# A decoder layer on one core: stores of h spread over more slots, v instead of silu multiplied by the norm factors on VectorE, form loads issued by SyncE

## The chip, the cores and the metric

The kernel runs on one core of one Trainium2 chip. The time is device microseconds of that core for one launch. The kernel before takes 2357.27 us, the median of 3 runs (2357.1 to 2358.58).

## What is computed

One layer of a hybrid decoder for 512 prompt rows and 8 sample rows (520 columns, held transposed: channels on partitions). A mixer (short convolution and gated linear attention) and its output projection come first; the change doesn't touch them. Then comes the ConvFFN, cut here to what matters:

```
xn = rmsnorm(x)                     # row factor R, gain g
u, v = split(xn @ w_up, 2)          # 2048 -> 2 x 5632
cu, new = causal_dwconv(u, prev, conv_w)   # width 3, over the rows
h = silu(cu + conv_b) * v
y = rmsnorm(x + h @ w_down)         # 5632 -> 2048
```

`new` is the last two rows of u (10 columns per channel here: 2 of the prompt and 8 samples), an output of its own.

## The kernel before, in words

**The stages.** Mixer and output projection run until about 866 us of the span, the up projection until 1867, the down projection until 2280, and the last four blocks of it with the final norm until 2356.

**Every product is in three parts.** A weight tile of 128 x 1024 numbers is split into `hi` (rounded, ScalarE, line 1045) and `lo` (the rest, VectorE, line 1049), and each activation into hi and lo as well; hi·hi, hi·lo and lo·hi are added up in PSUM. The tags `hi` and `lo` have three buffers each.

**Both projections use a fast 2 x 2 scheme with seven products.** Instead of eight block products there are seven, of sums of weight blocks and sums of input blocks ("forms"). `order` lists them: for each of 44 groups t of the up projection (128 channels of u and of v) the products r = 1, 5, 6, 2, 7, 3, 4, then for each of 5 chunks c of the down projection's inputs and 4 groups g of its outputs the same seven. One product is 24 matmuls. I call the time of one product a slot; a group has 7 slots, j = 0 to 6, and two groups, an even t and the odd one after it, are a pair.

**One pass of the loop (line 1301) is one slot.** In this order it emits: `up_finish` of the product just done; the 24 matmuls; `prepare(i + 2)`, which makes hi and lo of the product two slots ahead and, where needed, the next weight sum into `s` or `raw` (VectorE, line 1009); the steps of `gate` that are due. TensorE, VectorE and ScalarE keep this order (class InOrder); SyncE's and GpSimd's instructions are placed by the scheduler, and each of those queues then works in its order too. All weight loads (`raw`) are issued by SyncE.

**up_finish.** After r = 2, 3 the two halves of u go to `zpad`, multiplied by R (lines 1124 to 1129), and `keep_last` copies the last ten columns to `last` (line 521, on GpSimd); after every eleventh group `last` is transposed by TensorE and stored as `flat`. After r = 7 and 4 the two halves of v come out, negated (lines 1126 and 1132).

**gate(t)** is a generator that starts in the group after t; the number it yields is the slot, counted from its start, at which it goes on. Slot 0: the convolution (line 459 on ScalarE, lines 464 and 467 on VectorE). Slot 1: silu (line 1159, ScalarE), then silu times R on GpSimd (line 1160, by the helper at 219). Slot 3: h = v · s (line 1163). Slot 4, for odd t: the sums t21 and t34 of the quarters of two groups' h (lines 1175 to 1178). Then `stored` writes hi and lo of four tiles to DRAM: b11 (a half of the even group's h) at slot 8, t21 at 10, t34 and h both at 11. The last four groups are stored plain.

**stored (line 1134)** makes hi in a tile `fh` (ScalarE, line 116; two buffers) and lo in place (VectorE, line 117), and GpSimd issues both as DMAs to `f_d` (line 1144).

**The down projection** loads its forms from `f_d` (line 1208, four loads of 260 KB a form) and the residual (`acc`, line 1221), both issued by GpSimd. `load_form(0, 0..3)` stands in the last up group, 4 to 6 in the first down group, and the forms of chunk c + 1 in the last group of chunk c, one in each slot.

Of the kernel before, what the change touches and what calls it, by code (L numbers as in the profile page):

```python
# [9 lines left out]
F32 = mybir.dt.float32  # L10
F32R = mybir.dt.float32r
U8 = mybir.dt.uint8
AF = mybir.ActivationFunctionType
ALU = mybir.AluOpType
# [3 lines left out]
P = 128  # L18
D = 2048
KD = D // P  # L20
NP = 512
NS = 8
T = NP + NS
HT = T // 2
# [5 lines left out]
CH = 4  # L30
NCD = 5
# [6 lines left out]
def trunk_kernel(  # L38
# [6 lines left out]
    nc = tc.nc  # L45
# [7 lines left out]
    dp = ctx.enter_context(tc.tile_pool(name="scratch", bufs=1, space=DRAM))  # L53
# [31 lines left out]
    def tmp():  # L85
        return tp.tile([P, T + 2], F32, tag="t", name="t")

    def two(ap):
        return ap.rearrange("p (a b) -> p a b", a=2)
# [24 lines left out]
    def split(src, hi, lo, scale=None):  # L114
        if scale is None:
            nc.scalar.activation(hi, src, AF.Copy)  # L116
            nc.vector.tensor_tensor(lo, src, hi.bitcast(F32), op=ALU.subtract)  # L117
        else:
            nc.scalar.activation(hi, src, AF.Copy, scale=scale)  # L119
            nc.vector.scalar_tensor_tensor(  # L120
                lo, src, scale, hi.bitcast(F32), op0=ALU.mult, op1=ALU.subtract
            )
# [95 lines left out]
    def ptt(out, a, b, op):  # L218
        nc.gpsimd.tensor_tensor(out, a, b, op=op)  # L219
# [40 lines left out]
    with ExitStack() as es:  # L260
# [67 lines left out]
        ps = tps()  # L328
# [184 lines left out]
        zcount[0] += 1  # L513
        return zpad[zcount[0] % 2]

    def keep_last(z, j, n, new_p, new_s, get=bank):

        jj = j % n
        if jj == 0:
            last[0] = zp.tile([P, 10, n], F32, tag=f"last{n}", name="last", bufs=2)  # L520
        nc.gpsimd.tensor_copy(last[0][:, :, jj], z[:, NP:])
        if jj == n - 1:
            lt, c0 = last[0], (j - n + 1) * P

            def out():
                ps = get()
                nc.tensor.transpose(
                    ps[: 10 * n, :P], lt.rearrange("p r j -> p (r j)"), idn
                )
                flat = zp.tile([110, P], F32, tag="flat", name="flat", bufs=2)  # L530
                nc.scalar.activation(flat[: 10 * n, :], ps[: 10 * n, :P], AF.Copy)
                for r in range(10):
                    dst = new_p[0, 0, r] if r < 2 else new_s[0, r - 2, 1]
                    nc.sync.dma_start(
                        dst[c0 : c0 + n * P].rearrange("(j p) -> j p", p=P),
                        flat[r * n : (r + 1) * n, :],
                    )

            soon.append(lambda: None)
            soon.append(out)  # L540
# [512 lines left out]
    def minus(out, ps, x):  # L1053
        nc.vector.scalar_tensor_tensor(out, ps, -1.0, x, op0=ALU.mult, op1=ALU.subtract)  # L1054

    def add(out, x, y):
        nc.vector.tensor_tensor(out, x, y, op=ALU.add)
# [31 lines left out]
    def up_finish(i):  # L1089

        _, (t,), r = order[i]
        st = state[t,]
        bk = st["bank"]
        if r == 1:
            st["z"] = next_z()
        z1, z2 = st["z"][:, 2 : 2 + HT], st["z"][:, 2 + HT : 2 + T]
        if r == 7:
            st["v"] = tmp()
            v1, v2 = halves(st["v"][:, :T])
        if not t:  # L1100
            if r == 1:
                st["c"] = tmp()[:, :HT]
                nc.scalar.activation(st["c"], bk["a"], AF.Copy)
            elif r == 2:
                add(z1, bk["e"], st["c"])
            elif r == 6:
                st["u"] = halves(tmp()[:, :T])
                add(st["u"][0], bk["b"], st["c"])
            elif r == 7:
                u3 = st["u"][1]  # L1110
                add(u3, bk["b"], st["c"])
                minus(v2, bk["c"], u3)
                minus(v1, bk["d"], u3)
            elif r == 3:
                add(z2, bk["c"], st["u"][0])
        elif r == 1:
            copied(st, "e")
        elif r == 6:
            copied(st, "f")
        elif r == 5:  # L1120
            st["c"] = tmp()[:, :HT]
            nc.scalar.activation(st["c"], bk["c"], AF.Copy)
        elif r == 2:
            nc.vector.tensor_tensor(z1, bk["e"], R[:, :HT], op=ALU.mult)
        elif r == 7:
            minus(v2, bk["a"], st["c"])
        elif r == 3:
            add(z2, bk["f"], st["c"])
            nc.vector.tensor_tensor(z2, z2, R[:, HT:], op=ALU.mult)
            keep_last(st["z"], t, 11, new_ffn_p, new_ffn_s, mm_bank)  # L1130
        elif r == 4:
            nc.scalar.activation(st["v"][:, :HT], bk["a"], AF.Copy, scale=-1.0)

    def stored(src, dst):

        n = src.shape[1]
        hi = wxp.tile([P, T], F32R, tag="fh", name="fh")[:, :n]
        lo = src.bitcast(F32R)
        split(src, hi, lo)
        for d, x in zip(dst, (hi, lo)):  # L1140
            if len(d.shape) == 3:
                x = two(x)
                d = d.rearrange("f p c -> p f c")
            nc.gpsimd.dma_start(d, x)

    def gate(t):

        st = state.pop((t,))
        z, v = st["z"], st["v"]
        if not t:  # L1150

            nc.vector.tensor_tensor(z[:, 2 : 2 + T], z[:, 2 : 2 + T], R, op=ALU.mult)
            keep_last(z, t, 11, new_ffn_p, new_ffn_s, mm_bank)
        c = tmp()
        conv_tap(c, z, fcw, NF, t, fcb[:, t : t + 1])
        conv_rest(c, z, fcw, NF, t, stf[:, t, :])
        yield 1
        s = tmp()
        nc.scalar.activation(s[:, :T], c[:, :T], AF.Silu)  # L1159
        ptt(s[:, :T], s[:, :T], R, ALU.mult)  # L1160
        yield 3
        h = tmp()[:, :T]
        nc.vector.tensor_tensor(h, v[:, :T], s[:, :T], op=ALU.mult)
        yield 4
        if t >= NF - CH:
            stored(h, hl_d[t - NF + CH])
            return
        if t % 2 == 0:
            even[t] = h
            return  # L1170
        he, dst = even.pop(t - 1), f_d[t // 8]
        i = t // 2 % 4
        t21, t34 = tmp()[:, :T], tmp()[:, :T]
        (b11, b12), (b21, b22), (t2, t1), (t3, t4) = map(halves, (he, h, t21, t34))
        nc.vector.tensor_tensor(t1, b11, b12, op=ALU.subtract)
        minus(t2, t1, b22)
        nc.vector.tensor_tensor(t3, b22, b12, op=ALU.subtract)
        minus(t4, t2, b21)
        yield 8
        stored(b11, [dst[6, x, i] for x in range(2)])  # L1180
        yield 10
        stored(t21, [dst[0:2, x, i] for x in range(2)])
        yield 11
        stored(t34, [dst[2:4, x, i] for x in range(2)])
        stored(h, [dst[4:6, x, i] for x in range(2)])

    f_d = [dp.tile([7, 2, 4, P, HT], F32R, name=f"f_d{c}") for c in range(NCD)]
    hl_d = [[dp.tile([P, T], F32R, name=f"h{s}_d{t}") for s in "hl"] for t in range(CH)]
    even = {}


# [6 lines left out]
    def load_form(c, j):  # L1198

        home = (7 * c + j) % 8  # L1200
        parts_ = []
        for x in range(2):
            tiles = []
            for q in range(2):
                t = slots[2 * home + q].tile(
                    [P, T], F32R, tag=f"y{'hl'[x]}{2 * home + q}", name="form"
                )
                nc.gpsimd.dma_start(
                    two(t), f_d[c][PLACE[ORDER[j]], x, 2 * q : 2 * q + 2].rearrange("i p c -> p i c")
                )  # L1210
                tiles += halves(t)
            parts_.append(tiles)
        xd[c, ORDER[j]] = list(zip(*parts_))

    def load_residual(g):

        for q in range(4):
            m, b = 4 * g + 2 * (q // 2), q % 2
            n = 4 * g + q
            acc[g, q] = bigA.tile([P, T], F32, tag=f"x{'hl'[n % 2]}{8 + n // 2}", name="acc")  # L1220
            nc.gpsimd.dma_start(
                two(acc[g, q]),
                x1_d[m : m + 2, :, b * HT : (b + 1) * HT].rearrange("m p c -> p m c"),
            )

    def load_last():

        for i in range(CH):
            for b, (t0, n) in enumerate(PARTS):
                q = []  # L1230
                for x in range(2):
                    t = quarter(bigA, f"x{'hl'[x]}{2 * i + b}", QW)[:, :n]
                    nc.gpsimd.dma_start(t, hl_d[i][x][:, t0 : t0 + n])
                    q.append([t])
                hs[b].append(q)

# [243 lines left out]
```

## Time and profile before

| what | value |
|---|---|
| median of 3 runs | 2357.27 us |
| the profiled execution's own time | 2357.82 us |
| its span, first to last instruction | 2356.1 us |
| granted TensorE clock, mean of the span | 0.973 |
| up projection, 866 to 1867 us | 1001 us, TensorE busy 933.63 |
| down projection, 1867 to 2280 us | 413 us, TensorE busy 405.77 |
| GpSimd's multiplications by R (line 219, 44) | 4846 ns each |
| `last` copies on GpSimd (line 521, 52 of which 8 in the mixer) | 987 ns each |

Times in a view are counted from the span's start. A wait is put down to the engine and line whose event came last. TensorE's busy time overlaps with its weight loads (PEld). The granted clock is a share of full speed; a busy TensorE at half the clock does half the work.

### The profile page before, as it was taken

To read this page: it belongs to the slowest core of one execution; us is meant where nothing else is said; L and a number is where in the kernel's file an instruction comes from. 1 tells how busy PE (TensorE), PEld (TensorE's weight loads), DVE (VectorE), ACT (ScalarE), POOL (GpSimd) and SP (SyncE) were. 2 spreads that over 40 slices of the span, in tenths; PEclk is the share of its full clock that TensorE was granted. 3 is DMA by queue.
4 is the path that set the end of the run, shared out by engine and by line. 5 is a ranking of instruction groups with operands and counts; after the bars stand their busy time and mean duration, and the time that the engine had idled before them with its cause. 6 is when DMAs were issued, how large, how long until landed. Compare 5 with 4: busy or idle time off the path is not lost.

```text
span 2356.1 us, 43650 instructions
## 1 busy us (share of the span) xinstructions
PE 2245.6 (95%) x18131; PEld 2218.8 (94%) x18131; DVE 1627.4 (69%) x2124; ACT 1003.6 (43%) x1385; POOL 675.3 (29%) x642
## 2 busy tenths in 40 slices
PE   8999999999999999999999999999998899999996
PEld 7998999999999999999989999999998899999996
DVE  6446456343334468888888888878887787888885
ACT  5334434321223345444544545444454444444445
POOL 2113223100002222433433334343343632321410
PEclk9999999999999999999999999999999999999998
DMA  7443334333455453655565465464556988866834
GB/s 215 116 121 117 102 109 127 93 90 91 118 157 167 153 173 108 155 121 139 127 149 131 115 163 132 120 153 122 140 129 155 236 240 220 235 175 167 217 108 135
DMA packets 481539, 344.06 MB, mean 146 GB/s; under 512 B 17673, under 2 KB 463525, under 8 KB 481197
## 3 DMA queue, kind: packets, MB, share of 16 engines
q1 hardware_dynamic: 396193, 246.70, 37.3%
q0 software_dynamic: 83824, 92.34, 16.8%
q8 instruction: 142, 2.33, 0.4%
q10 hardware_dynamic: 1324, 2.23, 0.3%
q14 instruction: 56, 0.46, 0.1%
HBM read 278.15 MB, written 63.27 MB: 145 GB/s over the span
## 4 chain that ended last, share of the span: by engine, by line
PE 68%; DVE 11%; DMA 8%; issue 6%; ACT 4%; POOL 3%; SPq 0%; DVEq 0%; ACTq 0%; POOLq 0%
PE mm L133 31%; PE mm L1077 15%; PE x L1253 6%; PE y L1253 6%; DMA f_d<-fh 5%; DVE lo L1049 4%; PE f L1253 2%; PE e L1253 2%; PE ms L1077 2%; DVE s L1009 2%; POOL t L219 2%; ACT hi L1045 2%; DVE t L1054 1%; PE ms L717 1%; DMA raw<-in_w_in_dram 1%
## 5 line engine op out<-in xcount | busy, mean ns | idle before, releaser
L1077 PE MATMUL mm<-yh,hi 128*128 128x260 f32 x1408 | 416.1, 296 | 61.3 <-DVE t L1054 61.3
L1077 PE MATMUL mm<-yl,hi 128*128 128x260 f32 x1408 | 414.8, 295 | 1.0 <-DVE yl L117 1.0
L1077 PE MATMUL mm<-yh,lo 128*128 128x260 f32 x1408 | 413.0, 293 | 0.0
L1049 DVE TENSOR_TENSOR lo<-s,hi 128x1024 fp32r<-128x1024 f32 x192 | 260.3, 1356 | 128.6 <-ACT hi L1045 128.2
L1045 ACT ACTIVATE hi<-raw 128x1024 fp32r<-128x1024 f32 x256 | 270.4, 1056 | 172.9 <-issue 59.4
L1077 PEld LDWEIGHTS mm<-yh,hi 128*128 128x128 f32 x1408 | 280.8, 199 | 65.0 <-ACT hi L1045 65.0
L1049 DVE TENSOR_TENSOR lo<-raw,hi 128x1024 fp32r<-128x1024 f32 x256 | 319.2, 1247 | 19.4 <-ACT hi L1045 18.2
L104 ACT ACTIVATE hi<-raw 128x1024 fp32r<-128x1024 f32 (+1 forms) x148 | 152.8, 1034 | 391.4 <-PE mm L133 380.8
L105 DVE TENSOR_TENSOR lo<-raw,hi 128x1024 fp32r<-128x1024 f32 (+1 forms) x148 | 185.9, 1258 | 192.4 <-ACT hi L104 182.6
L133 PE MATMUL mm<-xh,hi 128*128 128x260 f32 (+2 forms) x1280 | 313.6, 294 | 5.0 <-ACT xh L119 2.6
L133 PE MATMUL mm<-xh,lo 128*128 128x260 f32 (+2 forms) x1280 | 303.6, 285 | 0.0
L133 PE MATMUL mm<-xl,hi 128*128 128x260 f32 (+2 forms) x1280 | 302.2, 284 | 0.8 <-DVE xl L120 0.5
L1077 PEld LDWEIGHTS mm<-yl,hi 128*128 128x128 f32 x1408 | 281.5, 200 | 1.3 <-DVE yl L117 1.2
L1077 PEld LDWEIGHTS mm<-yh,lo 128*128 128x128 f32 x1408 | 281.9, 200 | 0.0
L1045 ACT ACTIVATE hi<-s 128x1024 fp32r<-128x1024 f32 x192 | 203.1, 1058 | 184.0 <-DVE s L1009 102.0
L219 POOL TENSOR_TENSOR t<-t,R 128x520 f32<-128x520 f32 x44 | 213.2, 4846 | 142.3 <-ACT t L1159 142.2
L133 PEld LDWEIGHTS mm<-xh,hi 128*128 128x128 f32 x1280 | 216.9, 190 | 15.4 <-issue 9.2
L133 PEld LDWEIGHTS mm<-xl,hi 128*128 128x128 f32 x1280 | 217.4, 190 | 1.6 <-DVE xl L120 1.4
L133 PEld LDWEIGHTS mm<-xh,lo 128*128 128x128 f32 x1280 | 215.9, 189 | 0.1
L1077 PE MATMUL ms<-xh,hi 128*128 128x260 f32 x704 | 198.9, 282 | 2.1 <-ACT xh L116 2.1
L1077 PE MATMUL ms<-xl,hi 128*128 128x260 f32 x704 | 198.4, 282 | 0.5 <-DVE xl L117 0.5
L1077 PE MATMUL ms<-xh,lo 128*128 128x260 f32 x704 | 198.9, 283 | 0.0
(388 smaller groups left out, 5401.1 us busy)
## 6 DMA issues: line engine op xcount, KB each, us to landing
raw<-in_w_up_dram SPq DMA_DIRECT2D x176, 512.0 KB
raw<-in_w_down_dram SPq DMA_DIRECT2D x96, 512.0 KB
raw<-in_w_in_dram SPq DMA_DIRECT2D x92, 512.0 KB
form<-f_d POOLq DMA_DIRECT2D x140, 260.0 KB, 7.5
f_d<-fh POOLq DMA_DIRECT2D x60, 260.0 KB, 5.6
f_d<-t POOLq DMA_DIRECT2D x60, 260.0 KB, 4.2
raw<-in_w_out_dram SPq DMA_DIRECT2D x28, 512.0 KB
xT_d<-t SPq DMA_DIRECT2D x16, 260.0 KB
```

Source lines behind the costliest of these rows:

```text
L104: nc.scalar.activation(hi, raw, AF.Copy)
L105: nc.vector.tensor_tensor(lo, raw, hi.bitcast(F32), op=ALU.subtract)
L133: nc.tensor.matmul(o, w, xx, start=first and i == 0, stop=last and i == 2)
L219: nc.gpsimd.tensor_tensor(out, a, b, op=op)
L717: nc.tensor.matmul(pb[:, c * 64 : (c + 1) * 64], L[:, c, :], rhs[:, c], start=True, stop=True,)
L1009: return lambda: nc.vector.tensor_tensor(out, x, y, op=ALU.add)
L1045: nc.scalar.activation(his[i], src, AF.Copy)
L1049: nc.vector.tensor_tensor(los[i], src, his[i].bitcast(F32), op=ALU.subtract)
L1054: nc.vector.scalar_tensor_tensor(out, ps, -1.0, x, op0=ALU.mult, op1=ALU.subtract)
L1077: nc.tensor.matmul(st["bank"][b], w[:, k, :], x, start=b not in st["used"] and k == 0 and j == 0, stop=k == 7 and j == 2, skip_group_check ...
L1253: nc.tensor.matmul(ps[:, m, :], w[:, k, m * P : (m + 1) * P], x, start=b not in st["used"] and k == 0 and j == 0, stop=k == 3 and j == 2, ...
```

## The change

**v times R on VectorE.** GpSimd's `s = silu · R` goes. In slot 2 VectorE multiplies v by R in place (128 x 520), and in slot 3 it makes h = (v · -1) · s by a scalar_tensor_tensor in place of a tensor_tensor. The sign moved there, so that the two halves of v are now taken out of PSUM without negation.

**The copy to `last`** of the up projection goes from GpSimd to ScalarE (the mixer's eight stay on GpSimd).

**Stores.** h is stored at slot 15 of the gate, that is in slot 1 of the second group after, no longer at 11 right behind t34.

**Loads.** The scratch tensors have type F32 instead of F32R (the same bytes), and the forms and the residual are loaded by SyncE. The last four groups' tiles (line 1233) are still loaded by GpSimd.

```diff
+        if get:
+            nc.scalar.activation(last[0][:, :, jj], z[:, NP:], AF.Copy)
+        else:
+            nc.gpsimd.tensor_copy(last[0][:, :, jj], z[:, NP:])
...
-            minus(v2, bk["a"], st["c"])
+            add(v2, bk["a"], st["c"])
...
-            nc.scalar.activation(st["v"][:, :HT], bk["a"], AF.Copy, scale=-1.0)
+            nc.scalar.activation(st["v"][:, :HT], bk["a"], AF.Copy)
...
         nc.scalar.activation(s[:, :T], c[:, :T], AF.Silu)
-        ptt(s[:, :T], s[:, :T], R, ALU.mult)
+        yield 2
+        nc.vector.tensor_tensor(v[:, :T], v[:, :T], R, op=ALU.mult)
         yield 3
+
         h = tmp()[:, :T]
-        nc.vector.tensor_tensor(h, v[:, :T], s[:, :T], op=ALU.mult)
+        nc.vector.scalar_tensor_tensor(h, v[:, :T], -1.0, s[:, :T], op0=ALU.mult, op1=ALU.mult)
...
         stored(t34, [dst[2:4, x, i] for x in range(2)])
+        yield 15
         stored(h, [dst[4:6, x, i] for x in range(2)])
...
-                nc.gpsimd.dma_start(
-                    two(t), f_d[c][PLACE[ORDER[j]], x, 2 * q : 2 * q + 2].rearrange("i p c -> p i c")
+                nc.sync.dma_start(
+                    two(t.bitcast(F32)),
+                    f_d[c][PLACE[ORDER[j]], x, 2 * q : 2 * q + 2].rearrange("i p c -> p i c"),
                 )
...
-            nc.gpsimd.dma_start(
+            nc.sync.dma_start(
                 two(acc[g, q]),
```

Where it moves instructions, three places. First GpSimd's queue over one pair in the middle of the up projection; `fh` rows are stores of hi, `t` rows of lo, 128x260 is b11, and 128x2x260 are t21, t34 and h. Before:

```order
L521 COPY last<-zpad_880 128x10
L219 TENSOR_TENSOR t<-t,R 128x520
L521 COPY last<-zpad_881 128x10
L1144 DMA f_d_9533<-fh 128x260
L219 TENSOR_TENSOR t<-t,R 128x520
L1144 DMA f_d_9533<-t 128x260
L1144 DMA f_d_9533<-fh 128x2x260
L1144 DMA f_d_9533<-t 128x2x260
L1144 DMA f_d_9533<-fh 128x2x260 x2
L1144 DMA f_d_9533<-t 128x2x260 x2
```

And now:

```order
L1146 DMA f_d_9531<-fh 128x260
L1146 DMA f_d_9531<-t 128x260
L1146 DMA f_d_9531<-fh 128x2x260 x2
L1146 DMA f_d_9531<-t 128x2x260 x2
L1146 DMA f_d_9531<-fh 128x2x260
L1146 DMA f_d_9531<-t 128x2x260
```

Only the eight stores are left; no multiplication and no copy stands between them.

Second, ScalarE at the border of two groups, from the last hi of weights for the old group to the convolution of the next gate. `hi<-s` behind `last` belongs to r = 5 of the next group, the one behind `t<-mm` to r = 6. Before:

```order
L116 ACTIVATE fh<-t 128x520 x2
L1045 ACTIVATE hi<-raw 128x1024
L1045 ACTIVATE hi<-s 128x1024
L1132 ACTIVATE t<-mm 128x260
L1045 ACTIVATE hi<-s 128x1024
L459 ACTIVATE t<-zpad_880,parf 128x520
```

And now:

```order
L116 ACTIVATE fh<-t 128x520
L1048 ACTIVATE hi<-raw 128x1024
L522 ACTIVATE last<-zpad_880 128x10
L1048 ACTIVATE hi<-s 128x1024
L1135 ACTIVATE t<-mm 128x260
L1048 ACTIVATE hi<-s 128x1024
L459 ACTIVATE t<-zpad_880,parf 128x520
```

The `fh` of h has gone from behind that of t34, and the copy to `last`, which reads `zpad` after VectorE's multiplication by R, stands ahead of the hi of r = 5.

Third, SyncE's queue where the down projection begins. Before:

```order
L1005 DMA raw<-in_w_up_dram 128x8x128 x36
L1005 DMA raw<-in_w_down_dram 128x4x256 x7
L534 DMA out_dram<-flat 11x128 x10
L1005 DMA raw<-in_w_down_dram 128x4x256 x73
L94 DMA raw<-in_w_down_dram 128x4x256 x15
```

And now:

```order
L1008 DMA raw<-in_w_down_dram 128x4x256 x3
L1213 DMA form<-f_d_9530 128x2x260 x3
L1008 DMA raw<-in_w_down_dram 128x4x256
L1213 DMA form<-f_d_9530 128x2x260 x13
L1008 DMA raw<-in_w_down_dram 128x4x256
L537 DMA out_dram<-flat 11x128 x10
L1008 DMA raw<-in_w_down_dram 128x4x256 x3
L1227 DMA acc<-x_d 128x2x260 x4
L1213 DMA form<-f_d_9530 128x2x260 x12
L1227 DMA acc<-x_d 128x2x260 x4
L1008 DMA raw<-in_w_down_dram 128x4x256 x4
L1213 DMA form<-f_d_9531 128x2x260 x4
```

Forms and residual now stand between the weights; the fifth to seventh form of the first chunk stand behind the ten stores of `flat`, three weight loads and four residual loads.

## Prediction before the run

> **What bounds the kernel now.** I read the engines' totals first, then busy times by stage, then the chain that ended last, then the waits, and at last VectorE's own timeline over one pair. Totals, from the page:
>
> ```profile
> PE 2245.6 (95%) x18131; PEld 2218.8 (94%) x18131; DVE 1627.4 (69%) x2124; ACT 1003.6 (43%) x1385; POOL 675.3 (29%) x642
> ```
>
> TensorE is the bound, but 69% for VectorE is a mean over unlike stages. By stage (columns: us, busy times of PE, PEld, DVE, ACT, POOL, granted clock, DMA share, GB/s), the up and the down projection:
>
> ```profile
> 866.00:1867.00 1001.00, 933.63 (x7420) 928.80 (x7418) 836.64 (x1061) 489.06 (x672) 393.27 (x278) 0.96 0.56 136
> 1867.00:2280.00 413.00, 405.77 (x3366) 405.29 (x3367) 332.52 (x324) 173.36 (x190) 129.87 (x167) 0.99 0.74 201
> ```
>
> The down projection has little to give. The up projection has 67 us without a matmul, and its clock is below full. VectorE is busy there for 84%. The chain of work (start, us, what) shows the period: 20 stretches of this kind lie between these two starts, so 19 pairs take 864.63 us, 45.5 us each.
>
> ```profile
> 957.40 13.29 PE mm L1077 x96
> 1122.01 5.78 PE mm L1077 x48
> 1822.03 13.12 PE mm L1077 x96
> ```
>
> The middle row is undisturbed: 48 matmuls in 5.78 us, a slot of 2.89, so that TensorE alone needs 14 · 2.89 = 40.5 us a pair. 5.0 us a pair are lost. The chain in one pair shows where:
>
> ```profile
> 1260.51 0.65 ACT t L1159
> 1261.24 2.09 POOL t L219
> 1263.33 2.95 issue
> 1266.43 0.60 POOL f_d L1144
> 1267.03 7.31 DMA f_d<-fh
> 1274.42 0.65 ACT fh L116
> 1275.71 0.43 DVE t L1054
> 1276.28 14.46 PE mm L1077 x96
> ```
>
> GpSimd multiplies silu by R; the store of t21's hi queues behind that; it lands 7.3 us later; ScalarE, which wants t21's `fh` buffer for h, waits, and with it every hi behind it; VectorE and TensorE follow. The waits over the whole run (total, times, longest):
>
> ```profile
> ACT fh L116 <- DMA f_d<-fh: 106.9, 20, 6.4
> PEld mm L1077 <- ACT hi L1045: 65.0, 20, 4.2
> PE mm L1077 <- DVE t L1054: 63.5, 21, 4.0
> ```
>
> Twenty pairs, 3.25 us of idle TensorE each (the last two rows are the same time). The rest of the 5.0 is the clock:
>
> ```profile
> 1230.64:1276.28 45.64, 42.11 (x337) 41.92 (x337) 37.63 (x49) 21.92 (x30) 17.76 (x13) 0.95 0.57 134
> 1276.28:1322.79 46.51, 43.25 (x337) 43.07 (x337) 37.47 (x49) 21.70 (x30) 17.69 (x13) 0.94 0.55 131
> ```
>
> These are two pairs; 0.05 · 45.64 = 2.3 and 0.06 · 46.51 = 2.8 us of full-speed work are missing.
>
> **The change part by part.** *The stall goes.* Without the multiplication and with h four slots later, ScalarE wants t21's buffer 5 slots (14.4 us) after it was filled. The path is fh 0.65, issue 0.60, landing at most 7.31: 8.6 us. t34 wants b11's buffer after 3 slots, 8.7 us; b11 is half as large, so its path is shorter. The lo of h is read out until about 0.7 + 0.7 + 7.3 us after slot 1; the tile is wanted by v in slot 5, 11.5 us after. If all else had room, a pair would be 40.5 us.
>
> *VectorE becomes the next limit.* Rows of its timeline and ScalarE's, at the border of two groups and after (start, duration; in brackets its wait):
>
> ```profile
> 1300.36 0.43 DVE L1129 TENSOR_TENSOR zpad<-zpad,R 128x260 f32<-128x260 f32 x1
> 1300.71 1.22 DVE L1049 TENSOR_TENSOR lo<-s,hi 128x1024 fp32r<-128x1024 f32 x1
> 1301.96 1.23 DVE L1009 TENSOR_TENSOR s<-s,raw 128x1024 f32<-128x1024 f32 x1
> 1304.38 1.23 DVE L1049 TENSOR_TENSOR lo<-s,hi 128x1024 fp32r<-128x1024 f32 x1 [1.19 <-ACT hi L1045]
> 1305.52 0.75 DVE L464 SCALAR_TENSOR_TENSOR t<-zpad,parf,t 128x512 f32<-128x512 f32 x1
> 1312.29 2.07 DVE L1049 TENSOR_TENSOR lo<-s,hi 128x1024 fp32r<-128x1024 f32 x1 [0.21 <-ACT hi L1045]
> 1314.89 0.69 DVE L1163 TENSOR_TENSOR t<-t 128x520 f32<-128x520 f32 x1
> 1315.50 0.42 DVE L1124 TENSOR_TENSOR zpad<-ms,R 128x260 f32<-128x260 f32 x1
> ```
>
> ```profile
> 1303.28 1.06 ACT L1045 ACTIVATE hi<-s 128x1024 fp32r<-128x1024 f32 x1 [0.61 <-DVE s L1009]
> 1304.25 0.81 ACT L459 ACTIVATE t<-zpad,parf 128x520 f32<-128x520 f32 x1
> ```
>
> VectorE's busy time in this pair is 37.5 us (row 1276.28:1322.79 above; a union, overlaps counted once). Its path for a changed pair:
> - Less 0.85: the lo of 2.07 us ran beside GpSimd's multiplication, its like take 1.22.
> - Plus 2 · 0.61: v times R, priced by L1163 (same shape, two inputs in SBUF), from its start at 1314.89 to the next at 1315.50.
> - Plus 2 · 0.06: h as a scalar_tensor_tensor (L464 takes 0.75 for 512 columns, L1163 0.69 for 520).
> - Plus 2 · 1.19: the wait for the hi of r = 6, which needs s from VectorE; in each group, as now.
> - Plus 2 · 1.4, new: the copy to `last` on ScalarE. It reads what L1129 writes, and the hi of r = 5 is queued behind it; the lo of r = 5 is VectorE's next instruction. Today that lo starts while L1129 ends. Then it starts after a reaction of 0.09 (s ends at 1303.19, hi starts at 1303.28), the copy, a hi of 1.06 and 0.04 to the lo, less 0.09 overlap of ScalarE's instructions (1304.25 against 1304.34), with 0.08 more because VectorE's overlap is lost. The copy itself isn't in the trace on ScalarE; the nearest row is this one (columns: busy, mean ns):
>
> ```profile
> L635 ACT ACTIVATE asm<-t 128x8 f32<-128x8 f32 x4 | 0.8, 208 | 4.0 <-DVE t L627 4.0
> L521 POOL COPY last<-zpad 128x10 f32<-128x10 f32 x52 | 51.3, 987 | 224.0 <-DVE zpad L1129 220.1 <-DVE zpad L1152 3.5
> ```
>
> I take 0.21, for it has ScalarE's fixed part and almost the shape. The other end is GpSimd's 0.99 for the same copy.
>
> Sum: 37.5 - 0.85 + 1.22 + 0.12 + 2.38 + 2.8 = 43.2 us. VectorE never waits for TensorE on this path (its products run ahead of what it evacuates), so this is the period: 2.3 us a pair less than 45.5, times 20 = 46 us. With GpSimd's price for the copy the pair is 44.8 (14 us gained); with no new wait it is 40.5. Groups without the stores, at both ends, stay at TensorE's pace. Taking v without the negation costs nothing and brings nothing: the instructions stay, and 128x260 is 0.42 on VectorE with or without.
>
> *Where TensorE then waits.* 43.2 - 40.5 = 2.7 us a pair, in pieces of about 1 us, mostly in r = 2, whose lo comes behind the convolution. Do they lower the clock? The shortest stall of today's twenty didn't. Its wait, and the 7 us that hold it and the 7 us behind it:
>
> ```profile
> PE mm L1077 <- DVE t L1054: 1.7, 1, 1.7
> 1455.00:1462.00 7.00, 6.13 (x51) 6.17 (x52) 6.12 (x8) 2.77 (x4) 3.17 (x4) 1.00 0.73 166
> 1462.00:1469.00 7.00, 7.00 (x61) 7.00 (x59) 6.63 (x9) 5.01 (x9) 2.96 (x1) 1.00 0.17 47
> ```
>
> So at 1 us I count on full clock. The Trainium skill speaks against it: "TensorE: Matmul & The Clock Gate", section "A second HAM failure mode: psum-queue depth-cycling", says that frequent micro-idles between groups of matmuls can make the clock swing between half and full. This case's row of 1.7 us disagrees for a single wait; for one in each group no run here shows it yet. By the rule the pair would be that of the third rival below, by the row it is 43.2.
>
> *The border to the down projection.* Today (what waited for GpSimd's last copy; the granted clock; SyncE's stores of `flat`):
>
> ```profile
>   PE mm L527: 5.9, 1
> 1870.00:1885.00 15.00, 11.64 (x73) 11.36 (x74) 6.83 (x9) 5.83 (x9) 14.87 (x22) 0.68 1.41 360
> 1873.51 5.03 SPq L534 DMA_DIRECT2D out_dram<-flat  x10
> ```
>
> The copy was stuck behind form loads in GpSimd's queue: 5.9 us idle, and 0.32 · 15 = 4.8 us of clock. Both go. New is SyncE's order: behind ten `flat` stores come 3 weight loads of 512 KB, 4 residual loads and the fifth form's 4 loads of 260 KB each, 3.7 MB, 10.3 us at 360 GB/s. After the first down product starts: 0.7 for transpose and flat, 5.0, 10.3 = 16.0 us; the fifth form is due after 4 · 2.89 = 11.6. I count 4.4 us of wait and 2.5 of clock, net -3.8. The ends are -10.7 (no wait) and +1.
>
> *Forms on SyncE's queue later on.* Weights queue behind forms that wait for TensorE, in the last group of each of four chunks. Behind six forms (24 loads, 6.4 MB) and one weight tile come the first three tiles of the group after next, 8.5 MB in all, 24.7 us at the 344 GB/s of this stretch:
>
> ```profile
> 1950.00:1955.00 5.00, 5.00 (x44) 5.00 (x44) 4.38 (x5) 1.43 (x2) 2.14 (x3) 1.00 1.29 344
> ```
>
> They start in slot 1 of the chunk's last group and are wanted, two slots ahead of the second next group, in slot 12, 31.8 us later: hidden, with 7 us of room. If that cover is too small, each microsecond beyond it is paid four times.
>
> Sum against the profiled execution's own 2357.8: -46 - 3.8 = 2308; the median of the runs is 0.5 lower, which I leave aside.
>
> **The rivals.**
> - *TensorE stays the bound.* The copy's wait is hidden, because VectorE runs ahead by more than I count. For it: prepare works two slots ahead, and 43.2 less 2.8 is just TensorE's 40.5. Against it: the order puts the lo directly behind. 20 · 5.0 = 100 less, with the border 2254.
> - *SyncE's queue holds weights back.* At a rate lower by a third, 24.7 becomes 37 us, 5.3 beyond the slot 12; with 2.5 of clock 7.8 us at four borders: 2308 + 31 = 2339. Against it: the page's third part (packets, MB, share of 16 engines), by which SyncE's queue q1 takes 0.151% a MB and GpSimd's q0 0.182%:
>
> ```profile
> q1 hardware_dynamic: 396193, 246.70, 37.3%
> q0 software_dynamic: 83824, 92.34, 16.8%
> ```
>
> - *The short waits lower the clock, slower than before.* Place: TensorE's wait in r = 2 of each group. If each brings one spell that costs 2.8 us as today's stalls do, TensorE needs 20.25 + 2.8 = 23.05 a group, 46.1 a pair, 0.6 more than now: 2357.8 + 12 - 3.8 = 2366. It decides from a loss of 2.5 us a group on. Against it: the row at full clock after 1.7 us. This is where the rule of the Trainium skill named above would lead.
> - *The stall stays*, on t34's `fh` instead of h's: 8.7 us of room against up to 8.6. Then the pair stays at 45.5 and only the border is gained: 2354.
>
> **How the numbers follow.** Forecast 0.60, TensorE the bound 0.17, SyncE's queue 0.10, the clock 0.08, the stall stays 0.05. Time: 2308 us. The forecast's own range is 2292 to 2340 (a new wait of 1.0 to 2.2 us a group); to 2250 and 2340 the first two rivals are in and 0.13 is out. A measurement of this kernel tells 0.2% (4.7 us) from no change. Faster by more: 0.60 + 0.17 + 0.10 = 0.87; within: 0.05; slower: 0.08.
>
> **What would show it.** Right: ScalarE's wait for `f_d<-fh` near zero; pairs of 43 us; VectorE busy for (37.5 - 0.85 + 1.34) / 43.2 = 88% of them; its waits for hi up by some 60 us in all; TensorE waiting in short pieces for lo in r = 2; up-projection clock near 1.00; one wait of some 4 us early in the down projection. Wrong: pairs near 40.5 (the copy is hidden), a clock still below 0.97 without long waits (the rule holds), or new waits of TensorE at the borders of chunks.

## The result and the profile after

The changed kernel takes 2305.87 us (median of 4 runs, 2303.64 to 2307.02) where the kernel before takes 2357.18 on the same chip: a ratio of 0.978, 95% interval 0.9765 to 0.9799. The profiled execution took 2303.64 us, its span is 2301.9, the mean granted clock 0.990. Here and below the ratios and their intervals leave out single executions that took far longer than the others of the same kernel (the medians keep them).

Totals, then the up and the down projection and one pair (columns: us, busy times of PE, PEld, DVE, ACT, POOL, granted clock, DMA share, GB/s):

```profile
PE 2225.7 (97%) x18131; PEld 2189.2 (95%) x18131; DVE 1625.2 (71%) x2168; ACT 998.2 (43%) x1429; POOL 305.1 (13%) x398
```

```profile
866.00:1816.00 950.00, 915.06 (x7431) 900.00 (x7430) 834.17 (x1103) 484.28 (x717) 130.93 (x186) 1.00 0.54 145
1816.00:2230.00 414.00, 404.77 (x3363) 404.11 (x3362) 333.07 (x326) 171.75 (x187) 21.67 (x15) 0.99 0.63 197
1255.50:1298.20 42.70, 41.34 (x339) 40.62 (x338) 37.70 (x51) 21.56 (x32) 5.40 (x8) 1.00 0.53 143
```

The clock of the up projection is full again (1.00), and VectorE's busy time in a pair is hardly changed, 37.7 us, but of a shorter pair: 88%. The length of a pair is best read from the tile `flat`, which is written once in 11 groups; its row gives the first and the last start, 33 groups apart. Before and after:

```profile
L531 ACT ACTIVATE flat<-mm x4: 277/278/278, 1122.1 to 1873.2; 110x128 f32<-110x128 f32 x4
```

```profile
L534 ACT ACTIVATE flat<-mm x4: 256/258/278, 1109.7 to 1812.5; 110x128 f32<-110x128 f32 x4
```

751.1 / 16.5 = 45.5 us a pair before, 702.8 / 16.5 = 42.6 after. These two rows also split the gain: 60.7 us were won up to the last `flat` (5.9 of them the wait for GpSimd's last copy), and from there to the end of the span it is 2301.9 - 1812.5 = 489.4 us where it was 482.9: 6.5 were lost again.

What is waited for over the whole run (total, times, longest):

```profile
ACT last L522 <- DVE zpad L1132: 188.6, 43, 4.8
DVE lo L1052 <- ACT hi L1048: 159.2, 185, 1.7
PE ms L1080 <- DVE lo L1052: 25.7, 39, 0.7
ACT fh L116 <- DMA f_d<-fh: 6.6, 1, 6.6
```

Of ScalarE's twenty waits for a store of `fh` (106.9 us) one is left. TensorE waits in nearly every group (39 of 44) for lo in r = 2, for some 0.7 us each time. VectorE's path at the border of two groups, and ScalarE's instructions there (start, duration, and in brackets the wait):

```profile
1229.08 1.22 DVE L1012 TENSOR_TENSOR s<-raw 128x1024 f32<-128x1024 f32 x1
...
1231.81 0.43 DVE L1132 TENSOR_TENSOR zpad<-zpad,R 128x260 f32<-128x260 f32 x1
1233.46 1.22 DVE L1052 TENSOR_TENSOR lo<-s,hi 128x1024 fp32r<-128x1024 f32 x1 [1.23 <-ACT hi L1048]
...
1237.13 1.23 DVE L1052 TENSOR_TENSOR lo<-s,hi 128x1024 fp32r<-128x1024 f32 x1 [1.19 <-ACT hi L1048]
```

```profile
1232.27 0.22 ACT L522 ACTIVATE last<-zpad 128x10 f32<-128x10 f32 x1 [4.79 <-DVE zpad L1132]
1232.39 1.04 ACT L1048 ACTIVATE hi<-s 128x1024 fp32r<-128x1024 f32 x1
```

ScalarE stood idle for 4.79 us. The hi of r = 5 was queued right behind the small copy. What it needs from VectorE, the weight sum `s`, was done at 1230.30 (first row); but the copy ahead of it had to wait for L1132, and so the hi started only at 1232.39. VectorE then waited 1.23 us for that hi. The second wait, 1.19, was there before.

At the border to the down projection (SyncE's queue; TensorE's wait; DMA share and GB/s in the last two columns):

```profile
1812.83 7.77 SPq L537 DMA_DIRECT2D out_dram<-flat  x10
...
1824.91 10.25 SPq L1213 DMA_DIRECT2D form<-f_d  x12
```

```profile
PE x L1259 <- DMA form<-f_d: 8.4, 2, 6.7
```

```profile
1816.00:1824.00 8.00, 8.00 (x69) 8.00 (x68) 7.77 (x10) 5.68 (x8) 0.00 (x0) 1.00 0.45 137
1820.00:1840.00 20.00, 11.60 (x77) 11.13 (x77) 8.80 (x11) 5.17 (x7) 3.23 (x6) 0.74 0.95 313
```

TensorE waits 8.4 us for the fifth form, and by the granted clock 0.26 · 20 = 5.2 us of full-speed work are missing in these 20 us. About half of that costs nothing, since the time at half clock begins while TensorE still stands idle (from 1828 to 1832 us the clock is 0.53 and TensorE does nothing). While SyncE worked off the stores of `flat`, the DMA engines had a share of 0.45 and moved 137 GB/s.

### The profile page after: what moved, and what is told of

It is laid out like the page before. It is cut to its first block, busy times and chain, and to the rows that moved or that the text cites. A ratio compares the mean times of both kernels' runs of the same rounds, so it can differ in the third digit from the quotient of the medians.

```text
span 2301.9 us, 43686 instructions
## 1 busy us (share of the span) xinstructions
PE 2225.7 (97%) x18131; PEld 2189.2 (95%) x18131; DVE 1625.2 (71%) x2168; ACT 998.2 (43%) x1429; POOL 305.1 (13%) x398
## 3 DMA queue, kind: packets, MB, share of 16 engines
q10 hardware_dynamic: 1324, 2.23, 0.3%
## 4 chain that ended last, share of the span: by engine, by line
PE 55%; DVE 30%; issue 6%; ACT 5%; DMA 2%; POOL 1%; SPq 0%; ACTq 0%; DVEq 0%; POOLq 0%
PE mm L133 32%; DVE lo L1052 13%; PE y L1259 6%; PE x L1259 6%; DVE s L1012 6%; ACT hi L1048 4%; PE f L1259 2%; PE e L1259 2%; DVE raw L1012 2%; PE mm L1080 2%; DVE t L464 1%; DVE t L1167 1%; PE ms L720 1%; DVE t L117 1%; DVE zpad L1132 1%
## 5 line engine op out<-in xcount | busy, mean ns | idle before, releaser
L1080 PE MATMUL mm<-yh,hi 128*128 128x260 f32 x1408 | 402.4, 286 | 4.3 <-DVE t L1060 4.3
L1080 PE MATMUL mm<-yl,hi 128*128 128x260 f32 x1408 | 399.3, 284 | 0.0
L1080 PE MATMUL mm<-yh,lo 128*128 128x260 f32 x1408 | 398.4, 283 | 0.0
L1052 DVE TENSOR_TENSOR lo<-s,hi 128x1024 fp32r<-128x1024 f32 x192 | 238.6, 1243 | 147.4 <-ACT hi L1048 147.4
L1080 PEld LDWEIGHTS mm<-yh,hi 128*128 128x128 f32 x1408 | 265.3, 188 | 10.2 <-ACT hi L1048 4.5
L1080 PEld LDWEIGHTS mm<-yh,lo 128*128 128x128 f32 x1408 | 266.0, 189 | 0.0
L1080 PEld LDWEIGHTS mm<-yl,hi 128*128 128x128 f32 x1408 | 265.7, 189 | 0.0
L1080 PE MATMUL ms<-xh,lo 128*128 128x260 f32 x704 | 203.9, 290 | 25.8 <-DVE lo L1052 25.7
L1080 PEld LDWEIGHTS ms<-xh,lo 128*128 128x128 f32 x704 | 133.3, 189 | 34.0 <-DVE lo L1052 34.0
```

Of the source, the lines that this page charges most:

```text
L1052: nc.vector.tensor_tensor(los[i], src, his[i].bitcast(F32), op=ALU.subtract)
L1080: nc.tensor.matmul(st["bank"][b], w[:, k, :], x, start=b not in st["used"] and k == 0 and j == 0, stop=k == 7 and j == 2, skip_group_check ...
```

## The experiments

Theory 1 is the prediction's: the stall came from the slot of h's store, and now VectorE's path with the copy's wait bounds the up projection. (For the loads on SyncE and the border, theory 1 is what the expectation says of that place.) Each kernel was timed beside the kernel before on its own chip. That kernel's median was 2346.04 us on the chip of four of them (copy on GpSimd, copy behind the hi, later store alone, multiplication alone), 2342.13 on that of the control and the three behind it, 2344.07 for the nine copies and 2344.58 for the last one, so mostly the ratios and the pairs are compared. None of these kernels leaves out work.

**The copy to `last` back on GpSimd.**

```diff
-        if get:
-            nc.scalar.activation(last[0][:, :, jj], z[:, NP:], AF.Copy)
-        else:
-            nc.gpsimd.tensor_copy(last[0][:, :, jj], z[:, NP:])
+        nc.gpsimd.tensor_copy(last[0][:, :, jj], z[:, NP:])
```

> The changed kernel with the copy to `last` back on GpSimd, nothing else. Theory 1 (VectorE's path bounds the up projection, and the copy's wait of 1.2 us a group is part of it): the path of a pair becomes 42.7 - 2 x 1.2 = 40.3, so TensorE's own 40.5 bounds it; ScalarE's wait for `last` is gone, VectorE's waits for hi fall by some 50 us, TensorE's short waits for lo go; 20 pairs x 2.2 = 44 less, about 2260 us. Rival A (VectorE's total work, about 38 us of 42.7, or something else sets the pair, and the copy is hidden): pair within 0.3 of 42.7, 2300 to 2308 us. Rival B (GpSimd's 0.99 us copy delays a store, which is late again): 2285 to 2310 with a wait of ScalarE for `fh`.

Measured: 2258.20 us (4 runs), ratio 0.9628 [0.9609, 0.9647]. Its `flat` row, a pair of the middle, and VectorE's waits for hi from 960 to 1700 us, first here and then in the changed kernel:

```profile
L531 ACT ACTIVATE flat<-mm x4: 277/278/278, 1102.0 to 1768.7; 110x128 f32<-110x128 f32 x4
```

```profile
1255.50:1298.20 42.70, 42.70 (x359) 42.70 (x358) 40.08 (x53) 22.49 (x32) 7.80 (x10) 1.00 0.55 154
```

```profile
DVE lo L1049 <- ACT hi L1045: 44.1, 38, 1.2
```

```profile
DVE lo L1052 <- ACT hi L1048: 83.3, 69, 1.2
```

666.7 / 16.5 = 40.4 us a pair, and TensorE is busy for the whole of the window. One of VectorE's two waits a group has gone: 39 us in 17 pairs, 2.3 a pair. Theory 1 holds, and rivals A and B fall; ScalarE waits only once for a store of `fh`, for 4.3 us.

**The copy on ScalarE, but behind the hi of r = 5.** The copy is kept in a list and emitted after `prepare(i + 2)`.

```diff
-            nc.scalar.activation(last[0][:, :, jj], z[:, NP:], AF.Copy)
+            dst = last[0][:, :, jj]
+            behind.append(lambda: nc.scalar.activation(dst, z[:, NP:], AF.Copy))
...
         prepare(i + 2)
+        while behind:
+            behind.pop()()
```

> The changed kernel with the copy to `last` still on ScalarE, but emitted behind the hi of r = 5 instead of ahead of it. Theory 1 (what costs is the copy's place ahead of hi in ScalarE's queue): as with the copy on GpSimd, pair 40.3 to 40.6, about 2260 us. Rival A (the copy's work on ScalarE, or ScalarE's load, costs): no change, 2300 to 2308 us. If this one is fast and the one with GpSimd too, the place in the queue and not the engine is the cause.

Measured: 2257.48 us, ratio 0.9625 [0.9609, 0.9642]; a pair is 664.8 / 16.5 = 40.3 us. ScalarE and VectorE at the same place:

```profile
1233.74 1.06 ACT L1050 ACTIVATE hi<-s 128x1024 fp32r<-128x1024 f32 x1 [1.85 <-PE ms L1082]
1234.82 0.22 ACT L524 ACTIVATE last<-zpad 128x10 f32<-128x10 f32 x1
```

```profile
1234.36 0.43 DVE L1134 TENSOR_TENSOR zpad<-zpad,R 128x260 f32<-128x260 f32 x1
1234.83 1.23 DVE L1054 TENSOR_TENSOR lo<-s,hi 128x1024 fp32r<-128x1024 f32 x1
```

```profile
L536 ACT ACTIVATE flat<-mm x4: 277/277/277, 1098.5 to 1763.3; 110x128 f32<-110x128 f32 x4
```

The same instruction on the same engine, one place later: the lo starts as L1134 ends, and some 47 us of the run are gone (2257.5 against 2304.9 for the changed kernel on another chip; by the pairs 2.3 · 20 = 46). The cause is the order of a queue, not the engine or its load.

**Nine copies in place of one**, in the changed kernel: the loop `for _ in range(9):` around ScalarE's copy.

> The changed kernel with the copy to `last` done nine times in a row in each group of the up projection (the same ten columns to the same place). Eight copies more cost ScalarE 8 x 0.12 to 8 x 0.21 = 1.0 to 1.7 us a group ahead of the hi of r = 5. Theory 1 (VectorE's path takes the wait in full): pair 42.7 + 2.0 to 3.4 = 44.7 to 46.1, TensorE's short wait for lo 1.6 to 2.4 us a group, 2345 to 2375 us if the clock stays full. Rival A (there is slack): pair below 44, under 2330. On the clock: if short waits in each group lower it, spells at half clock show here behind the waits of r = 2 and the pair goes on to 47 or more; in the changed kernel 0.6 to 0.75 us in each group didn't.

Measured: 2389.22 us, ratio 1.0189 [1.0168, 1.0209]. ScalarE, VectorE's lo, the pair's window and the `flat` row:

```profile
1265.43 2.24 ACT L523 ACTIVATE last<-zpad 128x10 f32<-128x10 f32 x9 [4.83 <-DVE zpad L1133]
```

```profile
1268.64 1.23 DVE L1053 TENSOR_TENSOR lo<-s,hi 128x1024 fp32r<-128x1024 f32 x1 [3.24 <-ACT hi L1049]
```

```profile
1241.40:1287.98 46.58, 42.58 (x339) 40.90 (x338) 37.65 (x50) 25.11 (x48) 5.42 (x8) 1.00 0.47 130
```

```profile
L535 ACT ACTIVATE flat<-mm x4: 251/256/257, 1133.1 to 1898.2; 110x128 f32<-110x128 f32 x4
```

The wait grew by 2.01 us a group, the pair by 765.1 / 16.5 - 42.6 = 3.8: nearly microsecond for microsecond, as theory 1 has it. The pair and the time lie above the range expected, because a copy more costs 0.25 us ((2.24 - 0.22) / 8), not 0.12 to 0.21. The clock is full all the same, with 4.0 us a pair without a matmul, all in pieces under 0.8 us. So the rival of the prediction in which short waits lower the clock falls, at nearly three times the idle time of the changed kernel (42.70 - 41.34 = 1.4 us a pair). The rule of the Trainium skill behind it ("TensorE: Matmul & The Clock Gate", section "A second HAM failure mode: psum-queue depth-cycling") is not borne out by waits of this size here.

**Only the later store of h**, in the kernel before.

```diff
         stored(t34, [dst[2:4, x, i] for x in range(2)])
+        yield 15
         stored(h, [dst[4:6, x, i] for x in range(2)])
```

> The kernel before with only h's store at slot 15 of the gate. Theory 1 (the stall of each pair is h's `fh` one slot behind t21's store): ScalarE's 106.9 us of waits for the stores of `fh` fall below 20 us; the later store of h's lo still queues behind a multiplication of 5 us on GpSimd, so some other wait of up to 2 us a pair may show; pair 40.5 to 43, that is 2257 to 2310 us. Rival A (the 5 us multiplication ahead of the store in GpSimd's queue is the cause, not the slot of h): the waits of ScalarE stay above 70 us, 2345 to 2358 us.

Measured: 2315.30 us, ratio 0.9874 [0.9857, 0.989]; a pair is 722.9 / 16.5 = 43.8 us. ScalarE waits only once more for a store of `fh`, for 6.4 us. In place of these waits stands one of VectorE. GpSimd's queue, VectorE, VectorE's waits for that DMA from 960 to 1720 us, and the `flat` row:

```profile
1372.63 5.20 POOL L219 TENSOR_TENSOR t<-t,R 128x520 f32<-128x520 f32 x1 [0.60 <-issue]
1377.79 0.61 POOL L1144 DMA_DIRECT2D f_d<-t  x1
```

```profile
1384.49 0.43 DVE L1054 SCALAR_TENSOR_TENSOR t<-mm,t 128x260 f32<-128x260 f32 x1 [2.27 <-DMA f_d<-t]
```

```profile
DVE t L1054 <- DMA f_d<-t: 34.0, 32, 3.1
```

```profile
L531 ACT ACTIVATE flat<-mm x4: 252/253/277, 1108.3 to 1831.2; 110x128 f32<-110x128 f32 x4
```

The slot of h is the cause of the stall, rival A falls. But in both groups of a pair a store of lo stands behind a multiplication in GpSimd's queue: in the first now that of h, in the second that of b11, as before. The rows show b11's (128x260): its store is issued at 1377.79, behind 5.2 us of multiplication, and its tile, wanted by v, is free only at 1384.4. This wait comes in nearly every group (32 times in some 35), 2.0 us a pair on VectorE. With 39.1 us of busy time and 2.5 of waits for hi a pair, VectorE's path makes 43.6 us, and the pair came out 0.8 us above the range. TensorE idles with it, mostly for 1 to 2 us at a time (39.6 us in 32 waits), and the granted clock from 1000 to 1700 us is still 0.99, which speaks against the rival on the clock as well.

**Only the multiplication**, in the kernel before: v times R on VectorE and the signs, as in the change's diff.

> The kernel before with only the multiplication by R moved: v times R on VectorE, h as a scalar_tensor_tensor, v without negation; h is stored at slot 11 as before, `last` copied and forms loaded by GpSimd. Theory 1 (the slot of h is the cause): t21's hi lands up to 8.6 us after its `fh` starts, and h wants that buffer about 3.5 us after it, so ScalarE still waits some 5 us a pair less what the multiplication had added; ScalarE's waits for `fh` stay above 60 us, 2335 to 2357 us. Rival A (the multiplication is the cause): the waits vanish, 2265 to 2300 us.

Measured: 2341.14 us (10 runs), ratio 0.998 [0.997, 0.9989], 5 us of gain. Nearly all of its stall is there:

```profile
ACT fh L116 <- DMA f_d<-fh: 97.6, 21, 5.9
```

Here theory 1 holds. The two parts alone bring 0.0126 and 0.002 of the time; together, without the copy's wait (and with the loads on SyncE, which bring nothing by themselves), they bring 0.037. The later store alone meets the multiplication, and without it the early store still meets t21's.

**The changed kernel again**, as a control on the chip of the next three.

> The changed kernel itself, as a control on the chip of the three runs that follow. Both theories: ratio to the kernel before 0.978 as in the first measurement (0.977 to 0.980), pair 42.7, whatever this chip's own time for the kernel before.

Measured: 2304.93 us (5 runs), ratio 0.9838 [0.982, 0.9857]. The expectation missed: the changed kernel takes the same time as on the first chip, but the kernel before is faster here by 15 us. The next kernel has the stall of the kernel before, and hints at the place: ScalarE waits 98.4 us for stores of `fh` there, where it was 106.9 in the kernel before on the first chip, and such a store lands in 5.2 us by its median, where it was 5.6. That this makes the whole difference isn't shown.

**Only the loads on SyncE**, in the kernel before: `load_form` and `load_residual` by `nc.sync`, with scratch tensors in F32, as in the change's diff.

> The kernel before with only the loads of forms and residual issued by SyncE. Theory 1 (at the border this trades one wait for another: GpSimd's copy stuck behind form loads, 5.9 us, for the fifth form late in SyncE's queue, 8.4 us, each with some 5 us of clock): the up projection keeps its stall of 20 pairs, and the time stays within -1 to +5 us of the kernel before. Rival A (the loads on SyncE bring the 3.8 us that the prediction counted, or more): 3 to 11 us faster. Rival B (weights held back in SyncE's queue at the chunks' borders): over 10 us slower.

Measured: 2345.17 us (12 runs), ratio 1.0012 [1.0, 1.0023]. TensorE's waits at the border:

```profile
PE x L1253 <- DMA form<-f_d: 4.9, 2, 4.1
PE mm L527 <- POOL last L521: 2.1, 1, 2.1
```

One wait takes the place of the other, and nothing is gained. Rivals A and B fall; no wait stands at the borders of chunks.

**The border: `flat` on GpSimd, the fifth form ahead of the residual**, in the changed kernel.

```diff
-                    nc.sync.dma_start(
+                    q = nc.gpsimd if new_p is new_ffn_p and j == NF - 1 else nc.sync
+                    q.dma_start(
...
-                    load_residual(0)
-                    for x in (4, 5, 6):
+                    load_form(0, 4)
+                    load_residual(0)
+                    for x in (5, 6):
```

> The changed kernel with two moves at the border: the ten stores of the up projection's last `flat` issued by GpSimd, and the residual's first four loads emitted behind the fifth form. Theory 1 (the fifth form is late because it stands behind ten flat stores of 7.8 us and four residual loads of 2.5 us in SyncE's queue): the 8.4 us of waits and 5.1 us of half clock go, 10 to 13.5 us less than the changed kernel, about 2293 where that takes 2306. Rival A (the DMA engines' rate sets when the fifth form lands, whatever the order): under 4 us less.

Measured: 2302.87 us (median of 5), ratio 0.9829 [0.981, 0.9848], 2.1 us below the control, less than the intervals tell apart. The gain that theory 1 expected here didn't come:

```profile
PE f L1260 <- DMA form<-f_d: 4.7, 2, 3.1
```

```profile
1816.00:1824.00 8.00, 8.00 (x70) 8.00 (x69) 7.65 (x10) 5.67 (x9) 4.49 (x9) 1.00 1.08 353
1824.00:1836.00 12.00, 7.30 (x51) 6.85 (x50) 7.48 (x9) 3.30 (x4) 2.21 (x4) 0.89 1.10 364
```

The hole in the DMA load is filled (353 GB/s where it was 137), the fifth form is in time, and now the sixth is late, with full DMA engines. Rival A was right on the time and on the limit, the rate of the DMA engines; which form is late, the order did decide. The Trainium skill says ("DMA: Bandwidth & Descriptors", section "Issuing engines are not separate DMA queues") that loads from several issuing engines share the same 16 DMA engines, and that spreading them only saves issue time. The trace agrees: with the stores issued by another engine the wait fell only from 6.2 us in the control to 4.7. The issue time saved is not small here, though: the ten stores held SyncE's queue for 7.77 us in the changed kernel.

**All three mends**: the copy behind the hi of r = 5, the two moves at the border, and the plain stores of the last four groups at slot 6.

```diff
-        yield 4
+        yield 6 if t >= NF - CH else 4
         if t >= NF - CH:
```

> All three mends together: the copy to `last` behind the hi of r = 5, the two moves at the border, and the plain stores of h of the last four groups at slot 6 instead of 4 (where the first one meets t34's store of group 39). Theory 1: the 40.3 us pair of TensorE's own, no half clock at the border, the wait at group 40 gone; ratio to the kernel before 0.9625 - 0.005 (13 us of the border) - 0.001 (2.2 us at group 40) = 0.956 to 0.958, about 2253 us where the kernel before takes 2357. If the border's waits come back in another place: 0.961 to 0.963.

Measured: 2252.26 us (median of 5), ratio 0.9609 [0.9591, 0.9628]. The wait at group 40 is gone, the border still waits (4.5 us for forms in all, of which 3.6 here):

```profile
PE f L1263 <- DMA form<-f_d: 3.6, 2, 2.5
```

```profile
L536 ACT ACTIVATE flat<-mm x4: 277/277/278, 1101.0 to 1763.4; 110x128 f32<-110x128 f32 x4
```

It beats both kernels: 90 us less than the kernel before and 53 less than the changed one on the same chip. Its pair is 662.4 / 16.5 = 40.1 us, the pace of TensorE alone. The ratio came out above 0.958, partly because the border gave less, partly because the kernel before is faster on this chip.

**The residual behind all forms**, in the kernel with the three mends.

```diff
-                    load_form(0, 4)
-                    load_residual(0)
-                    for x in (5, 6):
+                    for x in (4, 5, 6):
                         load_form(0, x)
+                    load_residual(0)
```

> The kernel with all three mends, and the residual's first four loads behind all three remaining forms instead of behind the fifth. Theory 2 (formed after the two moves at the border brought only 2 us: the DMA engines are full at some 360 GB/s from 10 us ahead of the first down product to 30 us after it, so the last form lands when the bytes ahead of it are through): 1.06 MB less ahead of the sixth form are 2.9 us; TensorE's waits there, 4.5 us, fall to 1.5 to 2.5 and the half clock of 3.4 us may go; 2 to 4.5 us less than with the residual ahead of it, 2248 to 2250 us where that took 2252.3. Rival (the residual becomes late instead): TensorE or VectorE waits for `acc`, 2252 or more.

Measured: 2256.05 us (median of 5), ratio 0.9615 [0.9601, 0.9628]: no gain. VectorE's and TensorE's waits there, and the load of the DMA engines:

```profile
DVE acc L1277 <- DMA acc<-x_d: 8.8, 2, 8.3
PE x L1263 <- issue: 4.6, 1, 4.6
```

```profile
1760.00:1800.00 40.00, 33.37 (x254) 32.75 (x253) 27.14 (x32) 15.58 (x21) 9.46 (x18) 0.91 1.07 350
```

The rival held. TensorE's waits for forms did fall, from 4.5 us to 1.4; but VectorE waits for the residual until 1786.6 us, and TensorE stands idle from 1785.1 to 1789.7, which the view puts down to "issue" and I to VectorE's wait. For 40 us the engines move 350 GB/s; whatever is put last is late. An earlier start of these loads wasn't tried.

## Why the prediction was right, and where it was off

*The time.* Predicted 2308, measured 2305.9, and by the mechanism of the forecast. That the number came so near is partly luck: two errors of opposite sign, 8.8 us more gain in the up projection and 4.4 us less at the border, in part made up for each other.

*The stall.* That it comes from the slot of h's store is shown (the later store alone leaves one of ScalarE's twenty waits for `fh`, the multiplication alone leaves 97.6 of 106.9 us). That t34 and v then have room is shown for the whole change, with one exception that the prediction passed over. It held that the groups without the stores stay at TensorE's pace. But the plain store of group 40, at slot 4, meets t34's store of group 39, at slot 11, and the stall is there once more:

```profile
1765.27 0.64 ACT L116 ACTIVATE fh<-t 128x520 fp32r<-128x520 f32 x1 [6.60 <-DMA f_d<-fh]
```

```profile
PE mm L1080 <- DVE t L1060: 4.3, 1, 4.3
```

```profile
1766.00:1776.00 10.00, 8.88 (x62) 8.91 (x63) 7.52 (x9) 4.55 (x8) 1.86 (x3) 0.83 0.29 97
```

4.3 us idle and 0.17 · 10 = 1.7 of clock.

*VectorE as the next limit.* Right, and shown by the copy's place. The pair was predicted at 43.2 us and is 42.6. The copy's wait was sized at 1.4 and is 1.23, twice a pair. The busy time of a pair is 37.70 where 37.5 - 0.85 + 1.34 = 37.99 was counted; a part of that is h, whose scalar_tensor_tensor takes the 0.69 us of the tensor_tensor, not 0.06 more:

```profile
1244.76 0.69 DVE L1163 TENSOR_TENSOR t<-t,R 128x520 f32<-128x520 f32 x1
...
1247.11 0.69 DVE L1167 SCALAR_TENSOR_TENSOR t<-t 128x520 f32<-128x520 f32 x1
```

The gain up to the last `flat`, without the 5.9 of the copy, is 54.8 us instead of 46. The choice of ScalarE's row of 128x8 as the price of the copy, against GpSimd's 0.99, was right.

*VectorE's waits for hi* were to rise by 60 us in all. This sign didn't come: over the whole run they rose from 146.5 to 159.2, and from 63.2 to 83.3 between 960 and 1700 us. The new wait is there twice a pair (all 69 waits of that stretch are these two kinds, four a pair), but the prediction left out that other waits for hi, within the stalled pairs, would go out of the same total.

```profile
DVE lo L1049 <- ACT hi L1045: 63.2, 73, 1.6
```

*The clock.* Full in the up projection, as the forecast held: the third rival is refuted, up to the idle time of nine copies. From 900 us on its one time at half clock, 3.4 us, follows the wait at group 40.

*The border.* The step that failed is the one that counted 16.0 us from the first down product to the fifth form, and so 4.4 us of wait. It took SyncE's stores of `flat` at 5.03 us, as before; they took 7.77. And it let the loads behind them run at 360 GB/s from their first moment, 10.3 us; from the end of those stores (1820.6 us) to the end of TensorE's wait (1834.3) it was 13.7, with 113 GB/s from 1820 to 1824. So the fifth form was there 21.2 us after the first down product (1813.1), and the wait became 8.4 us (6.2 in the control). The 2.5 us of clock were near: of the 5.2 counted above about half falls on an idle TensorE (and so does a part of the 4.8 counted for the kernel before). Instead of -3.8 the border gave -5.9 + 6.5 = +0.6 us, and the loads on SyncE alone gave a ratio of 1.0012. What makes the stores of `flat` slower in their queue wasn't tried. With the hole behind them filled the DMA engines are full, and neither order of the loads tried was free.

*The other rivals.* TensorE as the bound (2254) was not the case, but it is what the copy one place later in its queue gives: 2257. Weights held back by forms in SyncE's queue at later chunks: no such wait in the traces. The stall on t34's `fh`: only at group 40.

## What to carry to other kernels

When a stall goes, follow the path of the next engine instruction by instruction, its waits included: VectorE at 84% busy became the limit because a copy of 0.22 us stood one place too early in an in-order queue of another engine, which cost 47 us. A small instruction that waits should stand behind the large one that doesn't. Two repairs can each look small alone (1.3% and 0.2%) and bring 3.7% together; and where the DMA engines are full, a new order only chooses what is late.

## What the runs showed of the hardware

- Idle pieces of TensorE under 0.8 us, 4.0 us in a pair of 46.6, left the granted clock at 1.00. Single idles of about 2 us went both ways. One of 2.23 us in the kernel with the copy behind the hi left it full (first two rows). In the kernel with only the multiplication moved, nineteen of twenty idles, 1.87 to 4.4 us each and 51.3 in all, were followed by 3.4 or 6.8 us at half clock, which brought the mean to 0.96 (last two rows); the twentieth, of 1.92 us at 1757 us, wasn't:

```profile
PE mm L1082 <- DVE t L1062: 2.2, 1, 2.2
```

```profile
1717.00:1724.00 7.00, 4.77 (x40) 4.58 (x39) 5.32 (x8) 3.21 (x5) 1.85 (x3) 1.00 0.66 199
```

```profile
PE mm L1077 <- DVE t L1057: 51.3, 20, 4.4
```

```profile
900.00:1800.00 900.00, 852.68 (x6822) 848.94 (x6821) 763.07 (x1009) 443.57 (x609) 148.53 (x197) 0.96 0.56 137
```

- The kernel before, which waits for its stores, took 2357, 2346, 2345, 2344 and 2342 us on five chips, the changed one, which hardly does, 2305.9 and 2304.9 us on two. That the waits make this difference isn't shown.
- Nine copies of 128x10 in a row on ScalarE, all to the same place, take 2.24 us, 0.25 for each one more, while the hi behind a single one starts 0.12 us after it.
